# Softmax attention of a two-layer encoder: normalising the outputs with the head dimension on the partitions

## The chip, the cores and the metric

The kernel runs on one core of one Trainium2 chip. That core has a matrix engine (TensorE, in the profile PE, with its weight loads as PEld), a vector engine (VectorE, DVE), an engine for pointwise functions (ScalarE, ACT), a general one (GpSimd, POOL), and a queue engine that issues DMAs (SyncE, SP). They run beside one another and wait for each other by semaphores. On-chip memory has 128 partitions; matmuls write to PSUM, a small memory of banks, and all else lies in SBUF. The metric is the time of one execution on the device, in microseconds (us), the median of several.

## The reference, cut to what matters

The program computes two layers over 1040 tokens (16 learned ones and 1024 of the input) of width 1024. Each layer has a linear-attention group (GLA), a softmax-attention group (FoX, 8 heads of 64), an output projection and a gated feed-forward part with a short convolution. The change touches only what comes after the softmax of the FoX heads:

```python
logits = (jnp.einsum('bqhd,bkhd->bhqk', q_b, kf)
          + c_b[..., None] - c_k[:, :, None, :])
logits = jnp.where(key_pos[None, :] <= q_pos[:, None], logits, -jnp.inf)
return jnp.einsum('bhqk,bkhd->bqhd', jax.nn.softmax(logits, axis=-1), vf)
...
o_fox = rms_norm(o_fox, fox_norm[i].reshape(FOX_HEADS, FOX_DH)).reshape(B, L, FOX_WIDTH)
h = h + jnp.concatenate([o_gla, o_fox], axis=-1) @ w_out[i]
```

Here `rms_norm(x, g)` is `x * rsqrt(mean(x*x) + EPS) * g` over the 64 numbers of a head. If N is the sum of exponentials times values and `den` the sum of exponentials, the softmax output is N / den, and its norm is N * rsqrt((sum(N*N) + 64 * EPS * den * den) / 64). So no division by `den` is needed, only its square under the root.

## The kernel before

All matrix products keep fp32 accuracy by splitting each operand into a rounded part (`hi`, type fp32r) and the remainder (`lo`): three matmuls per product (`mm3`, lines 256 to 258). The split is one ACT cast and one subtraction on DVE or POOL (`split`, lines 372 to 376; for weights lines 223 and 225).

Attention of a layer holds the tokens transposed, features on the partitions. `fox` runs over 4 head pairs `p` (two heads `e` each) and over the query tiles of 116 rows (the first one 112), in groups of two tiles: (7,8), (5,6), (3,4), (1,2), (0). One *step* `n` is one head and one tile: 72 steps a layer. A step computes scores on PE (lines 712 and 713), their minimum and the bias on DVE (line 715), the exponentials and their sum `den` on ACT (line 727). Two steps later the probabilities are transposed on PE (line 748) and split into `PT` (lines 372, 373); three steps later `fox_av` multiplies them with the values (line 774) into the one PSUM bank with the tag `av`. Its 128 partitions hold, for one head, the products with the rounded values in one half and with the remainders in the other, one column a query. ACT copies it to SBUF (`avs`, line 777).

When both heads of a group are through, `fox_fold` runs at step n + 4: it transposes the four (or two) pieces of `avs` back to queries on partitions (line 787), adds the halves (lines 790, 791), squares them (793), computes the inverse root per query and head on 4 columns (lines 795 to 798 and `rsqrt`, lines 307 to 311) and multiplies (802). At n + 6 `fox_store` transposes the result (line 813) so that features are on the partitions again, scales it by the gain and stores it to `mixd` (lines 820, 821, DMA from POOL's queue); for the last pair it splits it straight into the operand of the output projection (lines 375, 376).

`fox` lists such later pieces by step and name (`at`, `run`, `fox_schedule`). Between them it gives out a stock of other matmuls (`work`: the next pair's query, key and value products, the gate of the GLA group, and in the last quarter the output projection), spread evenly over the steps. The order of the engines' queues is made from this program order by a planner that simulates the program and lets a ready instruction go before one that is not. DMAs of SP stand in one queue: weights (`raw`, line 214), the copies `kA` and `kL` (line 638), the forget biases `cb` (line 863), `gog` (line 669). Buffers with one copy (`bufs=1`) are taken again when their last reader is through.

Of the kernel before, what the change touches and what calls it, by code (L numbers as in the profile page):

```python
# [10 lines left out]
F32 = mybir.dt.float32  # L11
F32R = mybir.dt.float32r
# [11 lines left out]
T = META + SEQ  # L24
# [143 lines left out]
class Kern:  # L168
    def __init__(self, ctx, tc, hT0, wm, wd, vec, wau, out):
# [26 lines left out]
        self.cd = dp.tile([8, T], F32, name="cd")  # L196
        self.later = []
# [554 lines left out]
    def fox_av(self, e, tiles, q, PT, avs, pp, part):  # L752
# [23 lines left out]
        if last < 4 * part + 4:  # L776
            nc.scalar.copy(avs[:, e, :width], av[:, :width])

    def fox_fold(self, tiles, avs, den, ap, pp):
        nc = self.nc  # L780
        nt = len(tiles)
        rows = self.rows_of(tiles[0])
        fo = pp.tile([128, 2, 2, 2, 64], F32, tag="S", name="fo")
        for ti in range(nt):
            for e in range(2):
                w = rows
                nc.tensor.transpose(fo[:w, ti, e].rearrange("p a b -> p (a b)"),
                                    avs[:, e, FT * ti:FT * ti + w], self.ident[:])
        f = ap.tile([128, 2, 2, 64], F32, tag="ff", name="ff", bufs=1)
        nc.scalar.copy(f[:rows, :nt], fo[:rows, :nt, :, 0])  # L790
        nc.vector.tensor_tensor(out=f[:rows, :nt], in0=fo[:rows, :nt, :, 1], in1=f[:rows, :nt], op=ALU.add)
        on = sq = ap.tile([128, 2, 2, 64], F32, tag="fon", name="fon", bufs=1)
        nc.scalar.activation(sq[:rows, :nt], f[:rows, :nt], AF.Square)
        vv, d2, y0, a = (ap.tile([128, 2, 2], F32, tag=f"f{x}", name=f"f{x}", bufs=2)[:rows, :nt] for x in "vdya")
        nc.vector.scalar_tensor_tensor(out=d2, in0=den[:rows, :nt], scalar=64.0 * EPS,
                                       in1=den[:rows, :nt], op0=ALU.mult, op1=ALU.mult)
        nc.vector.tensor_reduce(out=vv, in_=sq[:rows, :nt], axis=AX.X, op=ALU.add)
        nc.vector.tensor_tensor(out=vv, in0=vv, in1=d2, op=ALU.add)
        fl = (lambda x: x) if nt == 2 else (lambda x: x[:, 0, :])
        self.rsqrt(fl(y0), fl(vv), fl(y0), fl(a), scale=1.0 / 64)  # L800
        for ti in range(nt):
            nc.vector.tensor_tensor(out=on[:rows, ti], in0=f[:rows, ti],
                                    in1=y0[:, ti, :].unsqueeze(2).to_broadcast([rows, 2, 64]), op=ALU.mult)
        return on

    def fox_store(self, lyr, p, tiles, on, ap, pp, mix):
        nc = self.nc
        n = FT * (len(tiles) - 1) + self.rows_of(tiles[-1])
        tr = pp.tile([128, 4, 128], F32, tag="S", name="tr")
        trf = tr[:].rearrange("p a b -> p (a b)")  # L810
        for ti in range(len(tiles)):
            w = self.rows_of(tiles[ti])
            nc.tensor.transpose(trf[:, FT * ti:FT * ti + w],
                                on[:w, ti].rearrange("p a b -> p (a b)"), self.ident[:w, :w])
        c0 = self.start_of(tiles[0])
        if mix is not None:
            self.split(mix[0][:, c0:c0 + n], mix[1][:, c0:c0 + n], trf[:, :n], self.v(lyr, V_XN, p))
            return
        st = ap.tile([128, 2 * FT], F32, tag="fst", name="fst", bufs=1)
        nc.scalar.mul(st[:, :n], trf[:, :n], self.v(lyr, V_XN, p))  # L820
        nc.gpsimd.dma_start(self.mixd[4 + p][:, c0:c0 + n], st[:, :n])
# [1117 lines left out]
```

## Time and profile before

| | us |
|---|---|
| median of three runs | 2478.07 |
| lowest and highest | 2475.57, 2478.91 |
| profiled execution, its own time | 2479.26 |
| span of that execution, first to last instruction | 2477.3 |

The mean granted TensorE clock is 0.997. The page counts busy time of each engine and lists groups of instructions by source line, with their shapes (partitions x elements), count, busy time, mean length and the idle time of the engine before them. The line of a helper stands for all its callers, so `rsqrt` and `split` are told apart by the tile that they write. Matmuls are pipelined: the length of one is from its start to its modelled end, and the next may start before that end. Attention's softmax heads run at about 176 to 510 us for the first layer and 1400 to 1735 us for the second.

### The profile page before, as it was taken

To read this page: it belongs to the slowest core of one execution; us is meant where nothing else is said; L and a number is where in the kernel's file an instruction comes from. 1 tells how busy PE (TensorE), PEld (TensorE's weight loads), DVE (VectorE), ACT (ScalarE), POOL (GpSimd) and SP (SyncE) were. 2 spreads that over 40 slices of the span, in tenths; PEclk is the share of its full clock that TensorE was granted. 3 is DMA by queue.
4 is the path that set the end of the run, shared out by engine and by line. 5 is a ranking of instruction groups with operands and counts; after the bars stand their busy time and mean duration, and the time that the engine had idled before them with its cause. 6 is when DMAs were issued, how large, how long until landed. Compare 5 with 4: busy or idle time off the path is not lost.

```text
span 2477.3 us, 47313 instructions
## 1 busy us (share of the span) xinstructions
PE 2447.8 (99%) x18286; PEld 2365.1 (95%) x18286; DVE 1875.6 (76%) x3769; ACT 1321.2 (53%) x2857; POOL 384.0 (16%) x565
## 2 busy tenths in 40 slices
PE   9999999999999999999999999999999999999998
PEld 8999999999999999999999999999999999998887
DVE  7666776869988888865865666777699888887667
ACT  7345766646555555642643466666465555556433
POOL 2023433210000000100210234331100000001002
PEclk9999999999999999999999999999999999999999
DMA  4232134333322214764412222243423212247722
GB/s 135 73 84 75 43 95 130 125 125 102 120 75 81 88 68 143 197 153 136 128 41 75 77 79 73 68 146 108 148 82 111 91 65 90 82 149 180 214 72 87
DMA packets 121872, 261.00 MB, mean 105 GB/s; under 512 B 15136, under 2 KB 36896, under 8 KB 121648
## 3 DMA queue, kind: packets, MB, share of 16 engines
q1 hardware_dynamic: 97440, 182.81, 23.9%
q0 software_dynamic: 22336, 72.88, 10.4%
q8 instruction: 143, 2.34, 0.4%
q10 hardware_dynamic: 1872, 2.31, 0.3%
q14 instruction: 81, 0.66, 0.1%
HBM read 177.31 MB, written 67.85 MB: 99 GB/s over the span
## 4 chain that ended last, share of the span: by engine, by line
PE 66%; issue 16%; DVE 11%; ACT 4%; DMA 2%; POOL 1%; SPq 0%; DVEq 0%; POOLq 0%; ACTq 0%
PE mm L256 8%; PE mm L258 7%; PE mm L257 7%; PE up L257 5%; PE up L258 5%; PE up L256 5%; PE down L257 4%; PE down L256 4%; PE down L258 4%; PE av L774 3%; PE tr L748 2%; PE S L712 1%; ACT P L727 1%; DVE S L715 1%; PE S L713 1%
## 5 line engine op out<-in xcount | busy, mean ns | idle before, releaser
L257 PE MATMUL up<-x,lo 128*128 128x260 f32 x2240 | 632.9, 283 | 0.9 <-DVE lo L1156 0.8
L256 PE MATMUL up<-x,hi 128*128 128x260 f32 x2240 | 632.8, 283 | 0.1
L258 PE MATMUL up<-x,hi 128*128 128x260 f32 x2240 | 632.9, 283 | 0.0
L257 PEld LDWEIGHTS up<-x,lo 128*128 128x128 f32 x2240 | 421.7, 188 | 1.4 <-DVE lo L1156 1.3
L256 PEld LDWEIGHTS up<-x,hi 128*128 128x128 f32 x2240 | 421.6, 188 | 0.4 <-ACT hi L1155 0.3
L258 PEld LDWEIGHTS up<-x,hi 128*128 128x128 f32 x2240 | 421.9, 188 | 0.0
L1155 ACT CAST hi<-raw 128x512 fp32r<-128x512 f32 (+1 forms) x490 | 266.4, 553 | 209.2 <-PE up L258 90.9
L256 PE MATMUL mm<-xh,hi 128*128 128x348 f32 (+4 forms) x1056 | 362.0, 343 | 0.0
L1156 DVE TENSOR_TENSOR lo<-raw,hi 128x512 fp32r<-128x512 f32 (+1 forms) x490 | 286.8, 600 | 78.7 <-ACT hi L1155 78.0
L258 PE MATMUL mm<-xl,hi 128*128 128x348 f32 (+4 forms) x1056 | 340.6, 322 | 0.0
L257 PE MATMUL mm<-xh,lo 128*128 128x348 f32 (+4 forms) x1056 | 339.7, 322 | 0.0
L256 PEld LDWEIGHTS mm<-xh,hi 128*128 128x128 f32 x1056 | 200.5, 190 | 2.0 <-issue 1.4
L257 PEld LDWEIGHTS mm<-xh,lo 128*128 128x128 f32 x1056 | 200.4, 190 | 0.1
L258 PEld LDWEIGHTS mm<-xl,hi 128*128 128x128 f32 x1056 | 199.2, 189 | 0.1
L1137 DVE TENSOR_TENSOR raw<-raw,raw 128x512 f32<-128x512 f32 (+1 forms) x230 | 147.0, 648 | 32.4 <-DMA raw<-in_wd_dram 30.1
L727 ACT ACTIVATE P<-S,m 116x460 f32<-116x460 f32 (+2 forms) x224 | 125.1, 562 | 71.5 <-DVE m L715 68.4
L256 PE MATMUL down<-x,hi 128*128 128x260 f32 (+1 forms) x504 | 161.1, 320 | 0.7 <-DVE dg L1614 0.7
L257 PE MATMUL down<-x,lo 128*128 128x260 f32 (+1 forms) x504 | 161.2, 320 | 0.4 <-DVE lo L1156 0.4
L223 ACT CAST hi<-raw 128x512 fp32r<-128x512 f32 (+2 forms) x152 | 87.4, 576 | 138.4 <-PE mm L258 53.8
L258 PE MATMUL down<-x,hi 128*128 128x260 f32 (+1 forms) x504 | 161.1, 320 | 0.0
L373 DVE TENSOR_TENSOR PT<-tr,PT 116x464 fp32r<-116x464 f32 (+3 forms) x240 | 122.9, 515 | 48.8 <-ACT PT L372 47.3
L1416 POOL DMA_DIRECT2D actd<-cv x44 | 23.5, 535 | 736.9 <-DVE cv L1415 736.9
(313 smaller groups left out, 5960.5 us busy)
## 6 DMA issues: line engine op xcount, KB each, us to landing
raw<-in_wm_dram SPq DMA_DIRECT2D x330, 256.0 KB, 3.0
raw<-in_wd_dram SPq DMA_DIRECT2D x48, 256.0 KB, 4.7
actd<-cv POOLq DMA_DIRECT2D x22, 520.0 KB, 3.0
actd<-cv POOLq DMA_DIRECT2D x22, 512.0 KB, 3.1
cb<-cd SPq DMA_DIRECT2D x16, 520.0 KB, 4.2
hm<-h POOLq DMA_DIRECT2D x32, 260.0 KB, 3.7
kA<-kA SPq DMA_DIRECT2D x24, 260.0 KB, 4.2
kL<-kL SPq DMA_DIRECT2D x24, 260.0 KB, 4.8
```

The lines of the kernel that those rows point to most:

```text
L223: nc.scalar.copy(hi[:, :n, :], raw[:, :n, :])
L256: nc.tensor.matmul(ps, wh, xh[:, c0:c0 + n], start=first, stop=False, skip_group_check=more)
L257: nc.tensor.matmul(ps, wl, xh[:, c0:c0 + n], start=False, stop=False, skip_group_check=more)
L258: nc.tensor.matmul(ps, wh, xl[:, c0:c0 + n], start=False, stop=last, skip_group_check=more)
L373: nc.vector.tensor_tensor(out=lo, in0=src, in1=hi.bitcast(F32), op=ALU.subtract)
L712: nc.tensor.matmul(S[:rows, :n], q["qA"][e][:, qs], q["kA"][e][:, c0:k1], start=True, stop=False)
L727: nc.scalar.activation(P[:rows, :n], S[:rows, :n], AF.Exp, scale=-1.0, bias=m[:rows, nch - 1:nch], accum_out=(den if nch == 1 else d3[:row ...
L748: nc.tensor.transpose(tr[:w, 3 - j, :rows], P[:rows, o:o + w], id_)
L774: nc.tensor.matmul(av[:, a:b], w.rearrange("p a b -> p (a b)"), x, start=(t == ts[0] and part == 0 and i == 0), stop=(t == last and i == 1))
L1137: nc.vector.tensor_tensor(out=q[out][:, :nk, :], in0=q[a][:, :nk, :], in1=q[b][:, :nk, :], op=op)
L1155: nc.scalar.copy(hi[:, :nk, :], src[:, :nk, :])
L1156: nc.vector.tensor_tensor(out=lo[:, :nk, :], in0=src[:, :nk, :], in1=hi[:, :nk, :].bitcast(F32), op=ALU.subtract)
```

## The change

The output of a group stays as the matmul leaves it, with the head dimension on the partitions.

- `fox_heads` follows `fox_av` for each head: ACT copies the other half of the `av` bank (64 partitions) to SBUF and DVE adds it to the own half, into `O`, whose upper and lower 64 partitions are the two heads. After the second head ACT squares `O` and the square is split into `hi` and `lo`.
- `fox_den`, at step n + 1, squares the denominators (as line 795 did) and writes them to DRAM (`dd`) by two DMAs on SP's queue, 4 bytes an element.
- `fox_spread`, at n + 3, reads them back by two DMAs on SP's queue, each row to 64 partitions.
- `fox_norm`, at n + 5, takes the place of `fox_fold` and `fox_store`: two matmuls with `pair` (a matrix with ones in two 64 x 64 blocks) sum the squares over each head's partitions and leave the sum on all of them; DVE adds the spread denominators; `rsqrt` runs on 128 partitions x 232 (or 112) columns; DVE multiplies, with the gain, and POOL's queue stores the result; for the last pair it is multiplied, and split.

`pair` is written once a layer by four ACT operations. The scratch tiles `fq0`, `fq1`, `fq2` have one buffer each and are used by the copies, squares and the root in turn.

```diff
         if last < 4 * part + 4:
-            nc.scalar.copy(avs[:, e, :width], av[:, :width])
+            self.fox_heads(e, st, av, width, ap)
...
+    def fox_den(self, p, tiles, st, ap):
...
+        nc.vector.scalar_tensor_tensor(out=d2, in0=den, scalar=64.0 * EPS, in1=den, op0=ALU.mult, op1=ALU.mult)
+        for e in range(2):
+            to = self.dd[p][e, c0:c0 + nt * rows].rearrange("(a b) -> b a", b=rows)
+            nc.sync.dma_start(to, d2[:, :, e])
+
+    def fox_spread(self, p, tiles, st, ap):
...
+        st["d2"] = ap.tile([128, 2 * FT], F32, tag="fd2", name="fd2", bufs=1)
+        for e in range(2):
+            self.nc.sync.dma_start(st["d2"][64 * e:64 * e + 64, :nt * rows],
+                                   self.dd[p][e:e + 1, c0:c0 + nt * rows].to_broadcast([64, nt * rows]))
+
+    def fox_heads(self, e, st, av, width, ap):
...
+        if e == 0:
+            st["O"] = ap.tile([128, 2 * FT], F32, tag="fO", name="fO", bufs=2)
+        O = st["O"][:, :width]
+        t = ap.tile([128, 2 * FT], F32, tag="fq0", name="ft", bufs=1)
+        nc.scalar.copy(t[own, :width], av[oth, :width])
+        nc.vector.tensor_tensor(out=O[own], in0=av[own, :width], in1=t[own, :width], op=ALU.add)
+        if e:
+            sq, hi, lo = (ap.tile([128, 2 * FT], d, tag=f"fq{i}", name="fq", bufs=1)[:, :width]
+                          for i, d in enumerate((F32, F32R, F32R)))
+            nc.scalar.activation(sq, O, AF.Square)
+            self.split(hi, lo, sq)
+            st["sq"] = hi, lo
+
+    def fox_norm(self, lyr, p, tiles, st, ap, pp, mix):
...
+        ps = pp.tile([128, 512], F32, tag="S", name="fs")[:, :n]
+        for i, x in enumerate(st["sq"]):
+            nc.tensor.matmul(ps, self.pair[:], x, start=i == 0, stop=i == 1)
+        v, y0, a = (ap.tile([128, 2 * FT], F32, tag=f"fq{i}", name="fv", bufs=1)[:, :n] for i in range(3))
+        nc.vector.tensor_tensor(out=v, in0=ps, in1=st["d2"][:, :n], op=ALU.add)
+        self.rsqrt(y0, v, y0, a, scale=1.0 / 64)
...
         if mix is not None:
-            self.split(mix[0][:, c0:c0 + n], mix[1][:, c0:c0 + n], trf[:, :n], self.v(lyr, V_XN, p))
+            nc.vector.tensor_tensor(out=O, in0=O, in1=y0, op=ALU.mult)
+            self.split(mix[0][:, c0:c0 + n], mix[1][:, c0:c0 + n], O, gain)
             return
...
+        nc.vector.scalar_tensor_tensor(out=O, in0=O, scalar=gain, in1=y0, op0=ALU.mult, op1=ALU.mult)
+        nc.gpsimd.dma_start(self.mixd[4 + p][:, c0:c0 + n], O)
...
         if e == 1:
-            at(n + 4, "fold", fold)
-            at(n + 6, "store", store)
+            at(n + 1, "den", lambda: self.fox_den(p, tiles, st, ap))
+            at(n + 3, "spread", lambda: self.fox_spread(p, tiles, st, ap))
+            at(n + 5, "norm", norm)
```

68 lines of the change are left out of this document (20 added, 48 removed).

## The prediction

> **What bounds the kernel now.** I read the page first: busy times of the engines, then the table of stretches (busy time of each engine per stretch), then the waits of TensorE (PE).
>
> ```profile
> span 2477.3 us, 47313 instructions
> ...
> PE 2447.8 (99%) x18286; PEld 2365.1 (95%) x18286; DVE 1875.6 (76%) x3769; ACT 1321.2 (53%) x2857; POOL 384.0 (16%) x565
> ```
>
> PE is busy 99% of the span. A busy PE is not by itself a full PE, so the next view matters more. Attention (the softmax heads) runs in two stretches, about 176 to 510 us and 1400 to 1735 us. Columns: us, then busy us (instructions) of PE, PEld, DVE, ACT, POOL, then granted clock, DMA share, GB/s.
>
> ```profile
> core 0: us, PE busy (x) PEld busy (x) DVE busy (x) ACT busy (x) POOL busy (x), PEclk, DMA share, GB/s
> ...
> 260.00:340.00 80.00, 79.80 (x566) 77.42 (x564) 54.37 (x175) 51.25 (x157) 31.23 (x43) 1.00 0.27 79
> ...
> 420.00:500.00 80.00, 76.48 (x540) 74.06 (x540) 65.96 (x203) 53.18 (x158) 15.94 (x31) 1.00 0.35 110
> ...
> 1640.00:1720.00 80.00, 77.81 (x542) 74.76 (x542) 70.17 (x217) 58.54 (x177) 18.80 (x37) 0.98 0.39 123
> ```
>
> ```profile
> PE mm L258 <- DVE ml L373: 3.5, 2, 1.8
> ...
> PE tr L748 <- DVE PT L373: 1.2, 1, 1.2
> ...
> PE av L774 <- DVE PT L373: 0.7, 2, 0.4
> ```
>
> In the middle of attention PE stands still 0.2 us of 80, with VectorE (DVE) at 68% and ScalarE (ACT) at 64%. Only in the last quarter of each attention, where the output projection's operands are split too, is DVE at 82% (66.0 of 80) and 88% (70.2 of 80), and there PE waits for it (the three rows). So in attention time is PE issue time, and an engine beside it has room except in that last quarter.
>
> **What PE loses.** `fox_fold` makes four transposes for a two-tile group and two for a one-tile group, `fox_store` two and one. A layer has 4 head pairs with 4 two-tile groups and 1 one-tile group each.
>
> ```profile
> L787 PE MATMUL fo<-ident,avs x144: 270/272/323, 200.4 to 1730.1; 128*116 128x128 f32 x128, 128*112 128x128 f32 x16
> ```
> ```profile
> L813 PE MATMUL tr<-ident,fon x72: 259/262/267, 210.0 to 1734.7; 116*128 116x116 f32 x64, 112*128 112x112 f32 x8
> ```
>
> All 216 go. The 272 and 262 ns are from start to end of one pipelined instruction; what one holds PE for is the distance of starts, from the timeline where both kinds stand between ordinary matmuls:
>
> ```profile
> 500.87 0.37 PE L813 MATMUL tr<-ident,fon 116*128 116x116 f32 x2
> 501.07 0.38 PE L787 MATMUL fo<-ident,avs 128*112 128x128 f32 x2
> 501.21 0.36 PE L256 MATMUL mm<-mh,wl 128*128 128x256 f32 x1
> 501.41 0.28 PE L257 MATMUL mm<-mh,wl 128*128 128x256 f32 x1
> 501.53 0.28 PE L258 MATMUL mm<-ml,wl 128*128 128x256 f32 x1
> ```
>
> Four transposes start from 500.87; the next matmul starts at 501.21, but its successor comes 0.20 us later where 0.12 is usual (501.41 to 501.53), so 0.08 of the last transpose shows there. (0.34 + 0.08) / 4 = 0.105 us each; 216 x 0.105 = **22.7 us** removed.
>
> **What PE gains.** 40 groups x 2 fp32r matmuls on the ones matrix: 64 of 232 columns, 16 of 112. Nearest rows, same operand types, same widths, each with a weight load of its own:
>
> ```profile
> 205.36 0.80 PE L774 MATMUL av<-PT,V 116*128 116x232 f32 x6
> 205.99 0.48 PE L748 MATMUL tr<-ident,P 116*116 116x116 f32 x3
> ```
> ```profile
> 493.45 0.33 PE L774 MATMUL av<-PT,V 112*128 112x112 f32 x2
> 493.62 0.28 PE L748 MATMUL tr<-ident,P 112*112 112x112 f32 x1
> ```
>
> Six take 0.63 us: 0.105 each; the narrow ones 0.17 / 2 = 0.085. 64 x 0.105 + 16 x 0.085 = **8.1 us** added. Bounds: nothing hides a matmul on a full PE, so not below 80 x 0.085 = 6.8; and if each cost a whole latency as in the row of 272 ns, 80 x 0.272 = 21.8. I take 8.1, the row of the same kind. Net on PE: 22.7 - 8.1 = **14.6 us less**.
>
> The Trainium skill speaks against counting so: "TensorE: Matmul & The Clock Gate", Part 4, gives about 275 ns for a transpose in a kernel's context and lays it to access latency. The row's 272 ns agrees as a latency, the starts 0.105 apart do not agree as a price; by the page's figure an estimate of what goes would be 216 x 0.275 = 59 us.
>
> **DVE and ACT.** Mean ns by shape, in the first attention:
>
> ```profile
> L373 DVE TENSOR_TENSOR PT<-tr,PT 116x232 fp32r<-116x232 f32 x16 | 6.3, 392 | 2.9 <-ACT PT L372 2.7
> ...
> L802 DVE TENSOR_TENSOR fon<-ff,fy 116x128 f32<-116x128 f32 x32 | 7.8, 286 | 0.4
> L791 DVE TENSOR_TENSOR ff<-fo,ff 116x256 f32<-116x256 f32 x16 | 6.7, 421 | 6.2 <-ACT ff L790 5.8
> L797 DVE TENSOR_REDUCE fv<-fon 116x4 f32<-116x256 f32 x16 | 6.7, 419 | 4.2 <-ACT fon L793 4.2
> ...
> L798 DVE TENSOR_TENSOR fv<-fv,fd 116x4 f32<-116x4 f32 x16 | 3.9, 242 | 0.3
> ...
> L309 DVE SCALAR_TENSOR_TENSOR fa<-fy 116x4 f32<-116x4 f32 x16 | 2.6, 162 | 5.0 <-ACT fy L308 4.9
> ```
> ```profile
> L820 ACT ACTIVATE fst<-tr,vec 128x232 f32<-128x232 f32 x12 | 5.4, 453 | 5.3 <-PE tr L813 5.3
> ...
> L676 ACT ACTIVATE ge<-ge 128x348 f32<-128x348 f32 x8 | 4.0, 499 | 4.3 <-DVE ge L675 4.3
> ...
> L307 ACT ACTIVATE fy<-fv 116x4 f32<-116x4 f32 x16 | 3.3, 206 | 9.5 <-DVE fv L798 9.5
> ...
> L793 ACT ACTIVATE fon<-ff 116x256 f32<-116x256 f32 x16 | 6.8, 424 | 5.3 <-DVE ff L791 5.3
> L790 ACT COPY ff<-fo 116x256 f32<-116x256 f32 x16 | 6.0, 374 | 6.3 <-PE fo L787 3.6 <-PE av L774 2.3
> ```
>
> DVE, a two-tile group: out go the add 0.42, the reduce 0.42, the sum of squares and denominator 0.24, three steps of the inverse root on 4 columns 3 x 0.16, two multiplies 0.57: 2.1 us. In come, all 232 wide and so 0.39: two adds of the halves, the low part of the squares, the denominator's add, three steps of the inverse root, the last multiply: 8 x 0.39 = 3.1. So **+1.0 us a group** at most +40 us in all; the square of the denominator stays. ACT: out go 0.37 + 0.42 + 0.45 + 2 x 0.21 = 1.7; in come a square, a cast, Ln and Exp, not over 0.50 each by the 348-wide row, near 0.40 at 232: 1.6. The half-height copy that replaces the copy of `av` I cost at the same 0.37 (row below). For the last head pair ACT keeps a scaled cast, +0.4. `pair` is set up by four small ACT operations a layer, long before its first use. ACT is level.
>
> Where DVE has room (54.4 of 80 us, some 4 groups, +4) this is hidden: 58 of 78. In the last quarter it is not quite: 66 + 5 and 70 + 5 in some 78 us, 91% and 96%. There the split operands and the attention's own low parts (L373), on which PE waited above, stand behind the wider operations in DVE's order. Bounds: nothing, if the bursts do not meet, to 2 x 5 us, if every added microsecond shows. I take 1.5 a layer, **+3 us**.
>
> **Moved and added waits.** The `av` bank is now freed by an ACT copy and a DVE add instead of the copy alone: at least 0.39 us later. Two such copies and the next matmul into the bank:
>
> ```profile
> 190.72 0.37 ACT L777 COPY avs<-av 128x232 f32<-128x232 f32 x1
> ...
> 197.56 0.36 ACT L777 COPY avs<-av 128x232 f32<-128x232 f32 x1 [0.46 <-PE av L774]
> ```
> ```profile
> 191.75 0.39 PE L774 MATMUL av<-PT,V 116*128 116x256 f32 x1 [0.35 <-ACT PT L372]
> ...
> 202.47 0.86 PE L774 MATMUL av<-PT,V 116*128 116x256 f32 x6
> ```
>
> The usual slack is the second, 4.5 us; the first, 0.66, stands once a layer, at the start. **+0.6 us** (none to 2). The norm's first DVE add waits for the denominators' way: four DMAs a group on SP's queue, two that scatter 4-byte elements to DRAM and two that read them back over 64 partitions each. Queued behind that add on DVE are the score minima (L715) and low parts PE needs. On SP they stand among weight loads, `cb`, `kA`/`kL` copies and `gog` loads. The scatter is issued one step after the group's last scores, the spread two steps later, the norm two steps after that; 72 steps a layer fill some 320 us, so two steps are over 8 us. POOL's store of the result waits for DVE instead of ACT; its queue (weights' low parts) gets nothing longer. 160 DMAs cost PE nothing I can name: cost 0, cover some 8 us against these rows:
>
> ```profile
> SPq L214 <- POOL lo L225: 289.2, 38, 29.3
> ```
> ```profile
> cb<-cd SPq DMA_DIRECT2D x16, 520.0 KB, 4.2
> ```
>
> A spread landed in 4.2 us where 128 rows of 4 KB were read; a spread here is 64 rows of 928 B. No row shows a 4-byte data scatter from SP; I bound its landing by 2 and 8 us. Sum: -14.6 + 3 + 0.6 = **-11 us**. The profiled execution took 2479.3 us, 1.2 above the median of the three runs, so 2468 for it and **2467** for the median.
>
> "DMA: Bandwidth & Descriptors" of the Trainium skill (Specifications) says that transfers under 512 B are read, modified and written; the scatter's elements are that. No run here shows its price, and nothing above rests on it.
>
> **Rivals.** *DVE gives it back* (0.15): both last quarters become DVE-bound, each added microsecond shows: -14.6 + 10 + 0.6 = -4, 2474. For it: 88% busy. Against: bursts of splits end before most of the norms. A second push is visible in this row of 348-wide operations:
>
> ```profile
> L681 DVE SCALAR_TENSOR_TENSOR gy<-ge,gy x12: 505/520/1450, 252.6 to 456.1; 128x348 f32<-128x348 f32 x8, 128x344 f32<-128x344 f32 x4
> ```
>
> One took 0.93 over the median; six operations a group have two SBUF inputs, as had seven short ones before, so a lock of that kind grows with width, not count.
>
> *Better than the sum* (0.12): the 10 serial ACT-DVE steps of the fold were also what some PE waits hung on; no DVE loss, 2463, at most 2460 if the waits above shrink by half.
>
> *The denominators come late* (0.09, slower): SP waited for POOL up to 29.3 us at one weight load. If spreads are queued behind such a load, the DVE add waits in order and PE with it. It decides from 14.6 / 40 = 0.37 us of PE standstill a group; at 0.8 us, 40 x 0.8 = 32, less 14.6: +17, 2495. Against: two steps are slack, and weights run ahead; their first cast in this attention waits for no DMA:
>
> ```profile
> L223 ACT CAST hi<-raw 128x512 fp32r<-128x512 f32 x29 | 18.1, 625 | 2.5 <-POOL lo L225 1.2 <-PE mm L258 0.5
> ```
>
> *Latency is the price* (0.04): were a transpose worth its whole 272 and 262 ns, and a new matmul 279 as `av` shows, 39.2 + 18.9 - 22 = 36 less, 2442. The starts speak against it. The rule of Part 4 named above would come out this way.
>
> **Numbers.** The sum 0.60 at 2467, itself 2462 to 2472. A measurement here tells 0.2%, 5 us, from no change: faster below 2473. Faster = 0.60 + 0.12 + 0.04, less a little from the sum's edge: 0.75. Same: the DVE rival and that edge, 0.16. Slower 0.09. The range leaves out the late denominators and the latency case and half of the better one's depth: 2460 to 2476.
>
> **What would show it.** After: no `fo`, no `tr` from `fon`, 80 matmuls on `pair` about 0.105 us apart; each stretch of attention shorter by about 7 us; DVE some 18 us busier a layer. PE waits on DVE in the last quarter not above 6 us a layer. Wrong, if the norm's add waits for a DMA, if `av` waits for its bank, or if PE's new matmuls start over 0.2 us apart.

## The result: 5.6% slower, and where the profile after shows it

The changed kernel took **2614.55 us** (median of 6 runs, 2608.99 to 2627.47) where the kernel before took 2478.22: a ratio of 1.0558, 95% interval 1.0544 to 1.0571. That is 136 us more. Forecast were 11 us less. The first lines of its page:

```profile
span 2615.2 us, 47461 instructions
...
PE 2477.1 (95%) x18150; PEld 2376.3 (91%) x18150; DVE 1933.9 (74%) x3777; ACT 1336.0 (51%) x2835; POOL 385.7 (15%) x565
```

TensorE (PE) runs 136 matmuls fewer, as predicted (18286 to 18150), and its share falls from 99% to 95%: it stands still. DVE is busy 58 us longer, ScalarE 15 (the lengths of ScalarE's operations add up to 1494 us in both kernels; busy time counts a moment in which two overlap once). The stretches of the prediction again (same columns: PE, PEld, DVE, ACT, POOL, granted clock, DMA share, GB/s):

```profile
260.00:340.00 80.00, 73.11 (x481) 68.82 (x481) 54.90 (x148) 46.44 (x128) 27.37 (x38) 0.96 0.38 67
420.00:500.00 80.00, 60.63 (x376) 57.18 (x374) 43.94 (x131) 37.56 (x111) 18.11 (x29) 0.85 0.56 105
1640.00:1720.00 80.00, 62.63 (x396) 57.76 (x395) 50.42 (x143) 41.86 (x119) 22.69 (x32) 0.91 0.43 55
```

In the second line every engine works less than before (PE 60.6 instead of 76.5 of 80 us, DVE 43.9 instead of 66.0), while the DMA engines' share rises from 0.35 to 0.56 at no more GB/s (105 against 110). When all engines wait and the DMA engines are busier for the same bytes, the thing to look for is a transfer. The waits of PE and of DVE in the changed kernel (total us, times, longest):

```profile
PE S L713 <- ACT P L728: 46.4, 12, 10.6
PE av L775 <- DVE Vm L374: 22.7, 5, 9.4
PE av L775 <- DVE fO L807: 15.5, 6, 4.2
PE av L775 <- DVE PT L374: 14.1, 25, 1.5
```

```profile
DVE fO L807 <- DMA mixd<-fO: 60.6, 12, 12.6
DVE S L716 <- DMA cb<-cd: 37.7, 5, 10.3
...
DVE fv L823 <- DMA fd<-dd: 9.8, 5, 4.7
```

The wait between the two, that of ScalarE's exponentials for DVE's minima, after and then before:

```profile
ACT P L728 <- DVE m L716: 98.0, 38, 11.8
```
```profile
ACT P L727 <- DVE m L715: 68.4, 60, 2.7
```

PE waits for ScalarE's probabilities, these for DVE's minima, and these for the load of `cb`; or DVE's next sum of the halves (L807) waits until the store of two groups ago has landed, because `fO` has two buffers. DVE had no waits for `cb` or for an output's store before. The norm's own add, which reads the denominators (L823), waits least of the three. The timeline of DVE around one boundary between head pairs shows both kinds:

```profile
458.35 0.65 DVE L716 CUSTOM_DVE_ANT_0 S<-S,cb 116x460 f32<-116x460 f32 x1 [9.84 <-DMA cb<-cd]
...
474.18 0.27 DVE L807 TENSOR_TENSOR fO<-av,ft 64x112 f32<-64x112 f32 x1 [10.72 <-DMA mixd<-fO]
```

The same time on SP's queue (start, duration with waits):

```profile
439.47 1.53 SPq L789 DMA_DIRECT2D dd<-fd  x2
441.09 0.49 SPq L874 DMA_DIRECT2D cb<-cd  x1
...
447.39 10.60 SPq L795 DMA_DIRECT2D fd<-dd  x2
458.07 1.01 SPq L789 DMA_DIRECT2D dd<-fd  x2
```

The load of `cb` is issued at 441.09, right behind two scatters, and DVE can use it only at 458.35. It is not late in the queue; it is late in landing. Over the two attentions a `cb` load lands 12.3 us after its issue (before: 4.3; medians of 12, from the issue to the last increment of its semaphore). For the loads of `h` the DMA view gives the same (us at the end), after and then before:

```profile
h<-mixd POOLq DMA_DIRECT2D x10, 520.0 KB, 12.6
```
```profile
h<-mixd POOLq DMA_DIRECT2D x10, 520.0 KB, 4.5
```

Not all of the loss is standstill. In the trace the granted clock is either 1.0 or 0.5. It is 0.5, mostly behind PE's long waits, for 102 us of the two attentions in the changed kernel, for 3.4 us in the kernel without the scatters (no_scatter, below). At 0.5 the `av` matmuls of 112x232 start 0.213 us apart (median of 9), at 1.0 0.111. The same 18150 matmuls keep PE busy for 2477.1 us here and for 2448.7 there, so of the 100 us between these two profiled executions 28 are a longer busy time of the same matmuls and 72 are standstill.

### The profile page after: what moved, and what is told of

It reads as the page before. It is cut to its first block, busy times and chain, and to the rows that moved or that the text cites. A ratio compares the mean times of both kernels' runs of the same rounds, so it can differ in the third digit from the quotient of the medians.

```text
span 2615.2 us, 47461 instructions
## 1 busy us (share of the span) xinstructions
PE 2477.1 (95%) x18150; PEld 2376.3 (91%) x18150; DVE 1933.9 (74%) x3777; ACT 1336.0 (51%) x2835; POOL 385.7 (15%) x565
## 4 chain that ended last, share of the span: by engine, by line
PE 58%; issue 17%; DMA 9%; DVE 9%; ACT 4%; POOL 2%; SPq 0%; DVEq 0%; POOLq 0%; ACTq 0%
PE mm L257 5%; PE mm L259 5%; PE mm L258 5%; PE up L258 5%; PE up L259 5%; PE up L257 5%; PE down L257 4%; PE down L258 4%; PE down L259 4%; DMA mixd<-fO 4%; PE av L775 2%; DMA raw<-in_wm_dram 2%; PE tr L749 2%; PE wo L257 1%; PE wo L259 1%
## 5 line engine op out<-in xcount | busy, mean ns | idle before, releaser
L775 PE MATMUL av<-PT,V 116*128 116x256 f32 (+4 forms) x768 | 142.0, 292 | 57.4 <-DVE Vm L374 22.7
L775 PEld LDWEIGHTS av<-PT,V 116*128 116x128 f32 (+1 forms) x768 | 118.8, 200 | 71.0 <-issue 41.4
```

What stands on the lines that cost most here:

```text
L775: nc.tensor.matmul(av[:, a:b], w.rearrange("p a b -> p (a b)"), x, start=(t == ts[0] and part == 0 and i == 0), stop=(t == last and i == 1))
```

## The experiments

Two questions: what makes transfers late, and what the new norm costs without that. Times are medians; a time is compared by its ratio to the kernel before on the same chip.

### Which part of the denominators' way costs 95 us

**den_by_matmul**: no DMA at all; the denominators are spread over the partitions by one more fp32r matmul a tile.

```diff
-        nc.vector.tensor_tensor(out=v, in0=ps, in1=st["d2"][:, :n], op=ALU.add)
...
+        for ti, t in enumerate(tiles):
+            w = self.rows_of(t)
+            nc.tensor.matmul(ps[:, FT * ti:FT * ti + w], st["d2"][:w, ti].rearrange("p a b -> p (a b)"),
+                             self.identr[:w, :w], start=False, stop=ti == len(tiles) - 1)
```

> The changed kernel with no DMA for the denominators: their square, repeated over 64 columns, is the weight of one fp32r matmul on an identity per tile (72 in all, 116 columns), added to the sum of squares in the same PSUM bank. If the four DMAs a group are the cause of the 137 us, whatever way they act, this gives the sum that was predicted without them: 2478 - 14.6 + 72 x 0.06 = 2468 plus some us of VectorE, 2465 to 2476. If the wider root and the one-buffer scratch tiles are the cause, it stays above 2570.

Measured: 2520.51 us, 1.0185 (1.0168 to 1.0202). Neither: the DMAs cost some 92 us (1.0558 less 1.0185, of 2478), and 46 remain without any of them.

**no_scatter**, **scatter_unread** and **scatter_apart**: the spreads read a row of ones. In the first the scatters are gone, in the second they stay and nobody reads them, in the third they write the same 4-byte elements 64 B apart.

```diff
-                                   self.dd[p][e:e + 1, c0:c0 + nt * rows].to_broadcast([64, nt * rows]))
+                                   self.de[p][e:e + 1, c0:c0 + nt * rows].to_broadcast([64, nt * rows]))
```

And in scatter_apart alone:

```diff
-        self.dd = [dp.tile([2, T], F32, name=f"dd{p}") for p in range(4)]
+        self.dd = [dp.tile([2, T, 16], F32, name=f"dd{p}") for p in range(4)]
...
-            to = self.dd[p][e, c0:c0 + nt * rows].rearrange("(a b) -> b a", b=rows)
+            to = self.dd[p][e, c0:c0 + nt * rows, 0].rearrange("(a b) -> b a", b=rows)
```

> The changed kernel without the two scatters a group; the two spreads read a DRAM row of ones written at the start, so the denominators are left out. Scatter as the cause (by the queue or by the memory): 2465 to 2485. Spreads or the wider norm as the cause: above 2570.

> The scatters stay as they are, on SP's queue, but the spreads read the row of ones, so nothing waits for a scatter to land; the denominators' values are left out. If SP's queue behind the waiting spread is the cause (queue theory): as without the scatter, 2465 to 2490. If the scatter's small writes hold up other transfers for some 8 us each (memory theory): most of the loss stays, 2560 to 2610, with cb still landing after 10 us and more instead of 4.3.

> As the one before, with the 4-byte elements 64 bytes apart in DRAM instead of side by side; the denominators' values are left out. If neighbouring writes to one short row are what makes the landing slow (median 8.0 us in the changed kernel): landing falls to about 3 us and the time lies 30 us and more below the run before. If each small write has its price wherever it goes: no difference over 10 us. By the queue theory both are at 2465 to 2490.

| kernel | us | ratio to before | scatter lands | `cb` lands |
|---|---|---|---|---|
| no_scatter | 2519.46 | 1.0172 (1.0152 to 1.0193) | - | 4.5 us |
| scatter_unread | 2618.51 | 1.0572 (1.0551 to 1.0593) | 8.5 us | 12.1 us |
| scatter_apart | 2521.85 | 1.0182 (1.0161 to 1.0203) | 2.7 us | 4.7 us |

no_scatter is between its two forecasts: the scatters are the larger part, not the whole. scatter_unread is 8 us above the range of the memory theory, with `cb` landing as that says. It decides against the queue: no spread waits for a scatter there, and nothing is won. The late spread (row of 447.39 above) is another victim, not the cause. scatter_apart decides for the place of the writes: as many 4-byte packets, from the same instruction on the same queue at the same time, cost nothing when they are 64 B apart. Side by side in one short row they keep other transfers from landing for about 8 us on the median. What happens in the memory meanwhile no run shows.

**before_scatters** puts the 80 scatters, unread, into the kernel before, with its old norm.

```diff
+        for e in range(2):
+            to = self.dd[p][e, c0:c0 + nt * rows].rearrange("(a b) -> b a", b=rows)
+            nc.sync.dma_start(to, d2[:, :, e])
```

> The kernel before, with the 80 scatters of the changed kernel and nothing else: in the fold the square of the denominators is also written, element by element, to the same short DRAM rows; nobody reads them. Theory 'neighbouring writes freeze the memory': it needs nothing of the new norm, so other transfers land 8 us late here too; but the kernel before has no add that waits for the store of two groups ago, so only the waits for cb and the loads show: between 2500 and 2575 us, and cb lands in over 9 us instead of 4.2. Rival 'only together': the scatter hurts only beside the spreads and the norm: 2477 to 2483 us and cb in 4 to 5 us.

Measured: 2550.77 us, 1.0299 (1.0269 to 1.0330): +74, with a `cb` load landing in 14.5 us. The loads of `h` (DMA view) and the waits of DVE and PE in this kernel:

```profile
h<-mixd POOLq DMA_DIRECT2D x10, 520.0 KB, 14.0
```
```profile
DVE S L716 <- DMA cb<-cd: 60.3, 6, 14.7
```
```profile
PE S L713 <- ACT P L728: 55.2, 11, 13.6
```

Both numbers are where the first theory put them: the scatter needs nothing of the new norm to do its harm. It is smaller than in the changed kernel; the sum of the halves that waits for a store is absent here, which is a likely reason, but no run shows it.

### What a microsecond of DVE and of PE is worth

**before_wide_ops** and **before_reduces** add four unused DVE operations a group to the fold of the kernel before, once with two SBUF inputs, once with one.

```diff
+            nc.vector.scalar_tensor_tensor(out=xw[:rows], in0=self.vec[:rows, :156], scalar=y0[:, 0, 0:1],
+                                           in1=self.vec[:rows, :156], op0=ALU.mult, op1=ALU.mult)
```
```diff
+            nc.vector.tensor_reduce(out=xw[:rows], in_=self.vec[:rows, :208], axis=AX.X, op=ALU.add)
```

> The kernel before, with four more VectorE operations a group of 156 columns with two operands in on-chip memory, put where fox_fold has its root; their result is not used, and nothing else is changed. 4 x 0.31 = 1.24 us a group, 50 us of VectorE in all. Load theory: 20 us and more slower, 2498 and up. Scratch theory: less than 8 us slower, since VectorE has the room.

> The kernel before with four more DVE operations a group at the fold's root, as in before_wide_ops, but with one SBUF input (a reduce over 208 columns, about 0.37 us) instead of two; their result is used nowhere. DVE's work grows by some 55 to 60 us, hardly more or less than in before_wide_ops (+54.6, which gave 2505.8 us, +28). Theory 'load': it is the length of DVE's queue ahead of what TensorE waits for that shows, so the time is 2500 to 2508 us. Theory 'port': what showed were the holds of two-input operations by GpSimd, up to 1.4 us each in one piece; an operation that is never held costs nothing beside a full TensorE: 2478 to 2488 us.

Measured: 1.0117 (1.0097 to 1.0138), +29 us for 54.6 us more of DVE; and 1.0062 (1.0047 to 1.0078), +15 us for 47.2 more. The first is what its load theory says; the second lies between both expectations. The tile view of `xw` in each (min/median/max ns):

```profile
L803 DVE SCALAR_TENSOR_TENSOR xw<-vec,fy x160: 366/375/1393, 204.6 to 1763.0; 116x156 f32<-116x156 f32 x128, 112x156 f32<-112x156 f32 x32
```
```profile
L803 DVE TENSOR_REDUCE xw<-vec x160: 351/369/372, 173.0 to 1472.7; 116x1 f32<-116x208 f32 x128, 112x1 f32<-112x208 f32 x32
```

With one SBUF input this operation takes the same time (351 to 372 ns); with two, some take a microsecond longer. Even an operation that nothing waits for and nothing holds costs a third of the busy time that it adds (15 of 47 us), though DVE is busy 76% of the span; one that can be held costs half (29 of 55).

**before_less_pe**, **before_less_dve**, **before_less_both** cut the kernel before: 128 value matmuls fewer, the fold's DVE operations away, and both.

```diff
+                if i and t in (tiles[0], tiles[0] - 1) and len(tiles) == 2:
+                    continue
```
```diff
-        nc.vector.tensor_reduce(out=vv, in_=sq[:rows, :nt], axis=AX.X, op=ALU.add)
-        nc.vector.tensor_tensor(out=vv, in0=vv, in1=d2, op=ALU.add)
...
-        self.rsqrt(fl(y0), fl(vv), fl(y0), fl(a), scale=1.0 / 64)
-        for ti in range(nt):
-            nc.vector.tensor_tensor(out=on[:rows, ti], in0=f[:rows, ti],
-                                    in1=y0[:, ti, :].unsqueeze(2).to_broadcast([rows, 2, 64]), op=ALU.mult)
+        nc.scalar.activation(y0, d2, AF.Ln, scale=1.0 / 64)
+        nc.scalar.activation(y0, y0, AF.Exp, scale=-0.5)
```

> The kernel before with 128 of its value matmuls left out (the low part of the probabilities for two key tiles of every two-tile group), everything else in place: same DVE, ScalarE and DMA work, the same waits in front of the matmuls that stay. 128 x 0.105 to 0.12 = 13 to 15 us less TensorE work, as much as the forecast took from the transposes. Theory 'TensorE alone sets the time', the forecast's first step: 2463 to 2467 us. Theory 'TensorE and the chain through ScalarE and DVE share the bound': the matmuls then wait for their operands instead, 2470 to 2478 us.

> The kernel before without seven to eight DVE operations of the fold a group (reduce, sum with the denominator, the root's refinement, the two multiplies): the norm is left out, the squares go on in its place; ScalarE's, TensorE's and the DMAs' work stay. Some 1.6 us of DVE a group, 40 groups: 60 to 65 us less. Theory 'one slope': a microsecond of DVE is worth 0.33 to 0.5 in both directions: 2447 to 2458 us. Theory 'bound by both': TensorE is 98 per cent full in attention and takes over at once, so little comes out: 2466 to 2475 us.

> before_less_dve and before_less_pe together. Theory 'bound by both': with DVE out of the way the 13 to 15 us of TensorE work show nearly in full, so this is 10 to 14 us below before_less_dve, where the same cut alone won 2 to 3 us. Theory 'the matmuls left out were covered by something else' (a buffer, a transfer, the order): again only 2 to 4 us below before_less_dve.

| | TensorE as before | 128 matmuls fewer |
|---|---|---|
| DVE as before | 1 | 0.9993 (0.9984 to 1.0002), 2475.70 us |
| DVE 43 us less | 1.0002 (0.9993 to 1.0011), 2477.55 us | 0.9939 (0.9926 to 0.9953), 2462.98 us |

Either cut alone wins nothing that can be told; the two together win 15 us. before_less_pe is in the range of its second theory. before_less_dve is above both of its ranges, with 43 us less of busy DVE time where 60 to 65 were expected (the lengths of its operations add up to 62 us less). The engines' rows of before_less_dve and of before_less_both:

```profile
PE 2443.4 (99%) x18286; PEld 2361.9 (95%) x18286; DVE 1832.4 (74%) x3497; ACT 1321.9 (53%) x2857; POOL 385.9 (16%) x565
```
```profile
PE 2429.1 (99%) x18158; PEld 2346.5 (95%) x18158; DVE 1831.9 (74%) x3497; ACT 1320.3 (54%) x2857; POOL 386.6 (16%) x565
```

PE is 14.3 us less busy and the kernel 14.6 us shorter: with DVE lightened every microsecond of PE shows. In before_less_pe, with DVE's old work, PE is as much less busy as the page says (12 us), but waits on DVE's low parts and on ScalarE's casts grow in small pieces (waits of PE; the first was 1.2 us in one piece before):

```profile
PE tr L748 <- DVE PT L373: 3.6, 8, 0.6
...
PE av L776 <- DVE PT L373: 2.8, 10, 0.3
...
PE av L776 <- ACT PT L372: 1.7, 6, 0.3
```

One cell of the table is not what its row says. In before_less_pe DVE is busy 12 us longer than before (1887.7 against 1875.6) for the same 3769 operations. A step of the root and the multiply behind it now meet a POOL operation in six groups. The step's tile view before and in before_less_pe, and one such meeting:

```profile
L309 DVE SCALAR_TENSOR_TENSOR fa<-fy x40: 151/161/164, 204.3 to 1732.8; 116x4 f32<-116x4 f32 x32, 112x2 f32<-112x2 f32 x8
```
```profile
L309 DVE SCALAR_TENSOR_TENSOR fa<-fy x40: 150/161/1254, 202.4 to 1727.1; 116x4 f32<-116x4 f32 x32, 112x2 f32<-112x2 f32 x8
```
```profile
303.54 1.29 POOL L225 TENSOR_TENSOR lo<-raw,hi 128x512 fp32r<-128x512 f32 x1 [0.34 <-ACT hi L223]
...
303.60 1.25 DVE L309 SCALAR_TENSOR_TENSOR fa<-fy 116x4 f32<-116x4 f32 x1 [0.34 <-ACT fy L308]
```

By the price above (0.53) these 12 us of DVE would be worth some 6 us, an estimate. So of the 12 us that the cut should have won, a part may have gone to these holds, and the rest to a bound that PE and DVE share; the table does not tell the two apart.

### What the new norm costs without the scatter

These kernels start from no_scatter or den_by_matmul, some 43 to 46 us over the kernel before.

**halves_in_place** (from no_scatter): the copy of the halves goes straight into `O`, without scratch. **late_squares** (from no_scatter): the squares and their split stand one step later. **matmul_den_own_bank** (from den_by_matmul): halves in place, and the sums in a bank of the transposes instead of the scores.

```diff
-        nc.scalar.copy(t[own, :width], av[oth, :width])
-        nc.vector.tensor_tensor(out=O[own], in0=av[own, :width], in1=t[own, :width], op=ALU.add)
+        nc.scalar.copy(O[own], av[oth, :width])
+        nc.vector.tensor_tensor(out=O[own], in0=av[own, :width], in1=O[own], op=ALU.add)
```
```diff
+            at(n + 4, "sq", lambda: self.fox_squares(st, FT * (len(tiles) - 1) + self.rows_of(tiles[-1]), ap))
```
```diff
-        ps = pp.tile([128, 512], F32, tag="S", name="fs")[:, :n]
+        ps = pp.tile([128, 512], F32, tag="tr", name="fs")[:, :n]
```

> The kernel without the scatters (2519 us; the denominators are left out), but ScalarE copies the other half of av straight into O and VectorE adds in place, so the copy takes no scratch buffer. Scratch theory (the copy waits on ScalarE until the root of the group before has left the one buffer fq0, 21.7 us in 20 waits in the changed kernel, and the probabilities' casts stand behind it): 15 us and more faster, below 2505. Load theory (VectorE's wider root itself is in the way): within 8 us of 2519.

> As no_scatter (2519 us; spreads read a row of ones, denominators left out), but ScalarE's squares and their split are issued one step after the group's last value matmuls, just ahead of the norm of the group before, and not right behind the halves' sum. Theory 'order': the square, cast and low part stand ahead of the next probabilities' split on ScalarE and VectorE at the moment TensorE needs it, so moving them gives 2495 to 2510 us. Theory 'load': the same work has to be done in the same step budget wherever it stands: 2515 to 2523 us.

> The kernel with the denominators by a matmul (2520 us), with the halves added in place and the sum of squares in a bank of the tag tr instead of S. If the waits of PE for the S banks (13.4 us at the sum of squares, 7.5 us at the scores) and the scratch buffer are the loss: 2470 to 2490. Load theory: above 2505.

Measured: 2517.35 us, 1.0164 (1.0144 to 1.0185); 2516.08 us, 1.0157 (1.0142 to 1.0172); 2527.90 us, 1.0215 (1.0197 to 1.0232). All three are in the range of the load theory. Three misses for theories of order, scratch and banks: moving a wait gains at most a few microseconds, and in the last the wait only goes from the score banks to the transposes'. (halves_in_place is no clean test of the scratch: ScalarE's copy waits for the store of `O` instead, 14.6 us.)

**no_refinement** (from no_scatter) leaves the inverse root's three DVE operations out. **den_fewer_holds** (from den_by_matmul) keeps the whole computation, but puts the root into the sums' bank and takes its square on ScalarE.

```diff
-        self.rsqrt(y0, v, y0, a, scale=1.0 / 64)
+        nc.scalar.activation(y0, v, AF.Ln, scale=1.0 / 64)
+        nc.scalar.activation(y0, y0, AF.Exp, scale=-0.5)
```
```diff
+        ps, y0 = bank[:, :n], bank[:, 256:256 + n]
...
+        nc.scalar.activation(a, y0, AF.Square, scale=(0.5 / 64) ** 0.5)
+        nc.vector.tensor_tensor(out=a, in0=a, in1=ps, op=ALU.mult)
+        nc.vector.scalar_tensor_tensor(out=y0, in0=a, scalar=-1.5, in1=y0, op0=ALU.add, op1=ALU.mult)
```

> The kernel without the scatters (2519 us), and without the three VectorE operations that refine the inverse root (the refinement and the denominators are left out): 2 us less on VectorE a group. Load theory: 25 us and more faster, below 2495, since 3 x 0.6 us x 40 leave VectorE's queue. Scratch theory: also faster, as the buffers come free sooner, but by less than half of the loss, 2500 to 2512.

> As den_by_matmul (2520 us, the whole computation), with the inverse root in the sums' bank, its square taken on ScalarE and the sign carried by the halves' sum, the halves in place. A group has one DVE operation less and none of the norm's has two SBUF inputs but the squares' low part; TensorE's work is the same, ScalarE's 0.4 us a group longer. DVE: 40 x (0.54 + 2 x 0.15) = about 34 us less. Theory 'load and port': at 0.33 to 0.5 us a microsecond, 2503 to 2509 us. Theory 'chain': the ten serial steps of the norm set its waits, and a longer ScalarE makes up for a shorter DVE: 2515 to 2523 us.

Measured: 2499.24 us, 1.0091 (1.0071 to 1.0111), 20 us below no_scatter for 52 us less of DVE; 2508.95 us, 1.0124 (1.0110 to 1.0138), 15 us below den_by_matmul in ratio for 27 us less. The first lies between the ranges of its two theories, the second in that of load and port. What the three refinement operations cost DVE is seen in no_scatter's tile view of `fv` (min/median/max ns):

```profile
L315 DVE SCALAR_TENSOR_TENSOR fv<-fv x40: 274/401/865, 208.7 to 1773.8; 128x232 f32<-128x232 f32 x32, 128x112 f32<-128x112 f32 x8
L316 DVE TENSOR_TENSOR fv<-fv x40: 265/400/1502, 209.6 to 1774.1; 128x232 f32<-128x232 f32 x32, 128x112 f32<-128x112 f32 x8
L317 DVE SCALAR_TENSOR_TENSOR fv<-fv x40: 269/394/1057, 211.0 to 1774.4; 128x232 f32<-128x232 f32 x32, 128x112 f32<-128x112 f32 x8
```

The medians are the 0.39 us forecast; the longest is almost four times that. Of the 96 that are 232 wide, 49 overlap a POOL operation in time; the other 47 take at most 0.403 us. In den_by_matmul the middle one reads one operand from PSUM, and its longest is no longer than its usual length:

```profile
L310 DVE TENSOR_TENSOR fv<-fv,fs x40: 270/380/397, 208.8 to 1776.4; 128x232 f32<-128x232 f32 x32, 128x112 f32<-128x112 f32 x8
```

And the timeline of no_scatter shows one such hold from its cause to PE:

```profile
296.19 1.97 POOL L632 TENSOR_TENSOR qA<-qt,qA 64x348 fp32r<-64x348 f32 x2
...
296.51 0.86 DVE L315 SCALAR_TENSOR_TENSOR fv<-fv 128x232 f32<-128x232 f32 x1 [1.74 <-ACT fv L314]
...
297.41 1.01 DVE L316 TENSOR_TENSOR fv<-fv 128x232 f32<-128x232 f32 x1
...
298.46 0.35 ACT L808 COPY ft<-av 64x232 f32<-64x232 f32 x1 [1.64 <-DVE fv L316]
...
298.91 0.41 PE L754 MATMUL tr<-ident,P 116*116 116x116 f32 x2 [0.61 <-DVE PT L379]
```

While POOL works from 296.19 to 298.16, two DVE operations take 1.9 us instead of 0.8; the low part of the probabilities, queued behind them, comes late, and PE stands for 0.61 us. The Trainium skill has the rule, in "SBUF — State Buffer", section "Who interferes with whom": a DVE instruction with two SBUF inputs contends with a GpSimd instruction that reads SBUF, one with a single SBUF input does not, as long as it is not in one of the modes that use both ports. The rows of this norm agree (1502 against 397 ns at the longest); an operation of the gate with one SBUF input that is held all the same comes below.

**light_norm** (from den_by_matmul): the square is written as fp32r at once and summed by one matmul, no refinement. **light_in_bank**: the same with the root in the sums' bank and the halves in place. **light_less_dve**: light_norm with the denominators' square spread by ScalarE, its tile with two buffers, the halves in place, the root in the squares' buffer.

```diff
-            nc.scalar.activation(sq, O, AF.Square)
-            self.split(hi, lo, sq)
...
+            nc.scalar.activation(hi, O, AF.Square)
```
```diff
+        ps, y0 = bank[:, :n], bank[:, 256:256 + n]
```
```diff
-        nc.vector.scalar_tensor_tensor(out=st["d2"][:rows, :nt], in0=den, scalar=64.0 * EPS, in1=den,
-                                       op0=ALU.mult, op1=ALU.mult)
...
+        nc.scalar.activation(st["d2"][:rows, :nt], den, AF.Square, scale=(64.0 * EPS) ** 0.5)
```

> As den_by_matmul (2520 us), but the square is written as fp32r at once and summed by one matmul (the remainders of the squares are left out), and the root is Ln and Exp alone (its refinement is left out). A two-tile group loses four DVE operations (low part 0.39, three of the refinement near 0.39), a cast on ScalarE and one matmul. DVE's work is then near or below that of the kernel before. Theory 'load': 40 x 4 x 0.39 = 62 us less DVE at 0.4 to 0.5, and 4 us less TensorE: 2486 to 2494 us from 2520. If DVE's load is all that TensorE waits for, the transposes saved show as well and it ends at 2462 to 2474 us, below the kernel before. Theory 'order and banks': the norm's chain through a bank of its own remains, 2500 us or more.

> As light_norm (2479 us; remainders of the squares and the root's refinement left out), but the inverse root stands in the other half of the sums' PSUM bank, so the last multiply has one SBUF input and GpSimd cannot hold it, and the halves are added in place. Theory 'port': the last multiply's mean falls from 0.71 us (24 wide ones of it in the first form) to about 0.40, some 10 us of DVE in all, worth 4 to 5 us: 2472 to 2476 us. Theory 'chain': the number of steps and their order stay, so 2477 to 2480 us.

> As light_norm (2479 us; remainders of the squares and the root's refinement left out), with the denominators' square spread by ScalarE instead of DVE, its tile with two buffers, and the halves added in place: some 17 to 20 us less DVE work than before and light_norm, ScalarE 14 us more, TensorE's work as in light_norm, 10 us below before. Theory 'TensorE and DVE bound it together': before_less_both won 14.6 us with 13 to 15 us less TensorE and 60 less DVE; a third of that DVE cut lets 4 to 8 of the 10 us through: 2470 to 2476 us. Theory 'the new norm's chain has its own price': the longer ScalarE and the same number of steps keep it at 2478 to 2483 us.

Measured: 2479.33 us, 1.0004 (0.9994 to 1.0013); 2482.99 us, 1.0018 (1.0009 to 1.0026); 2499.04 us, 1.0088 (1.0075 to 1.0102). None is in a range of its theories: light_norm lies between two of them, the others above all of theirs. The engines' row of light_norm:

```profile
PE 2440.0 (98%) x18182; PEld 2351.4 (95%) x18182; DVE 1875.5 (76%) x3577; ACT 1320.1 (53%) x2797; POOL 384.7 (16%) x565
```

By the page its DVE and ScalarE are busy as long as before (1875.6 and 1321.2), PE 8 us less, and the time is the same, as in before_less_pe. light_in_bank shortened the held multiply (from 457 median and 1014 longest to 450 and 457 ns) and won nothing. light_less_dve missed by more: DVE 15 us less busy, ScalarE 17 more, and 21 us slower than light_norm. PE's waits name where:

```profile
PE fs L806 <- ACT P L727: 14.7, 12, 2.8
```

The sums' bank waits for ScalarE to read the scores out of it. Four of these waits are 2.7 to 2.8 us long, 11.0 of the 14.7 us. The timeline ahead of one of them:

```profile
263.79 1.87 DVE L675 TENSOR_SCALAR ge<-gx 128x348 f32<-128x348 f32 x1
...
264.15 1.30 POOL L225 TENSOR_TENSOR lo<-raw,hi 128x512 fp32r<-128x512 f32 x1
...
265.69 0.49 ACT L676 ACTIVATE ge<-ge 128x348 f32<-128x348 f32 x1 [1.91 <-DVE ge L675]
...
268.29 0.55 ACT L727 ACTIVATE P<-S,m 116x348 f32<-116x348 f32 x1
...
268.45 0.46 PE L806 MATMUL fs<-fq,pair 128*128 128x112 f32 x1 [2.78 <-ACT P L727]
```

The exponentials stand behind the gate of the GLA group, not behind a new square, and so do the minima that they need. Its DVE operation (L675, median 0.34 us, one SBUF input) takes 1.87 us beside a POOL operation, ScalarE waits 1.91 us for it, and PE 2.78 us. den_by_matmul, which has no new square on ScalarE, has four such waits of 2.4 us; in light_norm the same operation is held up to 2.55 us, but none of its waits at the sums is over 0.4 us. So light_less_dve does not tell what ScalarE's added work costs. None of these versions beats the kernel before; den_fewer_holds is the best that computes everything.

## Why the prediction was wrong, by its own steps

**The account.** Of the 136 us, 93 to 99 are the scatters (1.0558 less scatter_apart's 1.0182, and 1.0572 less 1.0172 in scatter_unread and no_scatter), by standstill and by the lower clock behind it. The other 43 are the norm itself (no_scatter). The forecast had nothing for the first and -11 for the second.

**"160 DMAs cost PE nothing I can name: cost 0, cover some 8 us"** is the step that failed most. The landing came out at the upper edge of its bounds (2 to 8 us; median 8.0, longest 17.5), and the cover held in the main: the add that reads the denominators waits 9.8 us in all, in five waits, though any such wait had been named as a sign of being wrong. What the step left out is that a DMA can hurt transfers that have nothing to do with it. The bound on a new kind of transfer was put on its own reader alone, and no bound was put on what else stands in the memory system. I named the Trainium skill's rule of "DMA: Bandwidth & Descriptors" (Specifications), that transfers under 512 B are read, modified and written, and said that nothing rested on it. The rule does not give this price either: scatter_apart's elements are as small and cost nothing that can be told (1.0182 against 1.0172). What counts is that they lie side by side.

**The rival "denominators come late"** had the sign, and a wrong mechanism: it had the norm's add wait behind SP's queue. In scatter_unread nothing reads what is scattered, and it is as slow.

**"So in attention time is PE issue time"** failed too, and with it the whole gain. The reading was: PE is busy 99% of the span and stands still 0.2 us of 80, DVE is at 68%. The two-by-two table shows what a full PE hides: 12 to 14 us less of it show only where DVE is lightened too. That PE and DVE's part of the chain end nearly together is the reading that fits; the longer holds of before_less_pe are a part of it that was not separated. Of the 14.6 us that the sum takes off PE about two thirds were there as work (10 us in no_scatter, from the distances of the starts in both attentions, with each distance across a wait put at the median of its kind: 307.7 and 309.2 us before, 304.4 and 302.6 there; the new matmuls start 0.110 apart, 0.105 was forecast). Nothing of it shows in the time: light_norm, with 8 us less of busy PE and no more of DVE, is level with the kernel before. The rival "latency is the price" falls with them.

**"Where DVE has room this is hidden: 58 of 78"**: not hidden. The two added-work runs price a microsecond of busy DVE at 0.33 (no holds) and 0.53 (with holds), no_refinement at 0.38. I took 3 of 40 us.

**DVE's size**: +1.0 us a group was forecast, 40 us in all; no_scatter's DVE is 62 us busier:

```profile
PE 2448.7 (97%) x18150; PEld 2350.4 (93%) x18150; DVE 1937.5 (77%) x3777; ACT 1333.1 (53%) x2835; POOL 404.6 (16%) x601
```

Three operations account for most of the difference: their means over both widths are 0.470, 0.653 and 0.485 us (40 each, 64 us), against 45 at the unheld lengths of 0.40 and 0.27. The price of 0.39 us came from a row that reads one operand from PSUM (L373, `PT` from `tr`); the refinement reads both from SBUF. The remark on a lock that "grows with width, not count" saw the hold and gave it no term in the sum. Lengths over the median of their kind add up to 20 us in the norm of no_scatter and to 3.6 us in the fold before. The narrow ones are no safer when they meet POOL (0.16 us became 1.25 in before_less_pe), they meet it less often: 24 of 160 before, 49 of the 96 wide ones in no_scatter. By the prices above 62 us of DVE are worth 20 to 33 of the 43.

**ScalarE level**: right. The group's ScalarE operations sum to 86.2 us before and 85.9 in no_scatter. **The `av` bank**: 0.6 us forecast; without the scatters PE waited 4.7 us for it in den_by_matmul and 0.2 in no_scatter.

**What stays open**: the 10 to 23 us between DVE's price and the norm's 43. In no_refinement DVE is only 10 us busier than before and the time still 23 us longer. light_norm, which also drops the squares' cast from ScalarE (40 of 0.367 us), is level. That points to ScalarE, ahead of the exponentials, as the third partner in the bound, but light_norm changes DVE and PE too; this is argued, not shown. The order of ScalarE's queue is another candidate: the four waits of den_by_matmul behind a held operation of the gate are 9.6 us of PE. No run takes these holds away alone. Nor was it tried which buffer ties the engines together (the probabilities' split tiles have one each).

## What to carry over

- An engine at 99% is not proof that its microseconds are the time's. Before taking a gain from a full engine, cut its work in one small run with all else in place; where nothing is won, the change has to lighten the next engine as well, and a change that lightens one and loads the other is likely to lose, as this one did.
- Do not scatter single 4-byte elements side by side into a short DRAM row in the middle of a kernel that streams. Give each its own 64 B, or spread the values with a matmul.
- When every engine is idler and the DMA share is up at the same GB/s, look at the landing times of transfers that the change did not touch.

## What the runs showed of the hardware that was not expected

- Neighbouring 4-byte writes (two DMAs of 232) land 8.0 us after issue on the median, though the packets of an undisturbed pair all start within 1 us of one another; 64 B apart they land in 2.7. Other transfers land later meanwhile: `cb` on SP's queue 12.3 instead of 4.3 us, `h` on POOL's 12.6 instead of 4.5.
- A 0.40 us DVE operation with two SBUF inputs took up to 1.50 beside a POOL operation; the one with an operand in PSUM never over 0.397. A TENSOR_SCALAR with one SBUF input (L675, 0.34 us) took up to 1.87 beside one in light_less_dve and 2.55 in light_norm.
- The granted clock was 1.0 or 0.5, nothing between, and 0.5 mostly behind long waits of PE: 0.85 on average in the stretch where PE was busy 60.6 of 80 us. A wait cost more than its length: 102 us of the two attentions ran at 0.5, and the same matmuls kept PE busy 28 us longer than in no_scatter.
